# When a linear-attention scan may begin: beside its own head's projections, or after them

## The chip, the cores and the metric

The kernel runs on one core of one Trainium2 chip. The metric is device time in microseconds of one execution, taken as the median of several runs. Engines are named as in the profile: PE (TensorE, matmuls), DVE (VectorE), ACT (ScalarE), POOL (GpSimd) and SP (SyncE, which issues most of the DMAs).

## The reference

One layer of a hybrid decoder trunk in float32, for 2048 tokens of width 1024 with 16 learned meta tokens in front. One normalised input `u` feeds two branches, a Mamba-2 scan (SSD, four groups of heads) and a gated linear attention (GLA, four heads of key width 128 and value width 256). Two sigmoid gates merge them and an output matrix follows.

```python
u = rmsnorm(hres, norm_w)
proj = u @ w_in                              # z, xbc, dt, q, k, v, g_gla, a_lr, merge gates
# GLA branch, per head: o_t = q_t S_t,  S_t = diag(a_t) S_{t-1} + k_t^T v_t
log_a = log_sigmoid(a_lr @ gla_gate_w2 + gla_gate_b) / 16
o = rmsnorm(gla_chunked(q * 128**-0.5, k, v, log_a), gla_norm_w)
y_gla = o * silu(g_gla)
merged = sum over branches of sigmoid(gate) * (branch @ w_branch)
out = rmsnorm(hres + merged @ w_out, final_norm_w)[:, 16:]
```

In `gla_chunked` the queries, keys and decays alone make the decayed keys and queries and the attention matrix within a chunk. The values `v` are multiplied in only afterwards, and the output gate `g_gla` only at the very end.

## The kernel before

There are two phases. **Phase 1** walks over four blocks of 512 tokens (`for b in range(nblk)`, L812). In each block it works through eight units one after the other: four SSD groups (`ssd_proj`, then `ssd_scan`) and four GLA heads (`gla_proj`, then `gla_scan`). A unit's projections are the bulk of PE's work. Every product is done in three float32r matmuls, high by high, high by low and low by high (`accum`, L175 to L179). **Phase 2** (L837 on) does the merge gates, the branch products and the output product from stored tiles, as sums of seven sub-products (`product`).

Inside phase 1 the projections and the scans are Python generators. Each `yield` of a projection runs one step of every scan in flight (`step`, L798), in the order in which they were begun. PE and SP keep exactly the order in which the program was written (`manual_schedule`, L811). The order on DVE, ACT and POOL is chosen by the framework's scheduler. So on PE the matmuls of a scan's step stand between two pieces of projection.

`gla_proj` of a head has six steps: queries q (24 matmuls of 512 columns), keys k (24), values in two halves (48 matmuls of 256 columns each), and the two output gates (24 each). `gla_scan` has eleven:

- step 1 makes the decayed keys `kd` and queries `qg` and starts the first level (`level_in(64)`); it has nothing on PE;
- step 2 transposes `kd` (L699), then the first `level_out` (L681);
- steps 3 and 4 hold two `level_out` each, step 5 one more and the diagonal sums (L745); a `level_out` is a pair of matmuls into one PSUM bank, which ACT or DVE then copies out (L685, L688);
- step 6 transposes half of the attention matrix (L760); steps 7 and 8 take the four chunks (L769 to L776) with the values, the state `s_gla` and a norm;
- steps 9 to 11 scale, transpose (L786), multiply by the gates `gs` (L787) and store (L790).

PSUM has eight banks in phase 1: three in pool `pj` (projections), three in `pt` (transposes and sums) and **two in `pc`**. From `pc` come the banks of `level_out`, those of the GLA chunks, and in `ssd_scan` two for each chunk in `after(c)`: `py` (L545) and `pst` (L549). On DVE, L555 and then L558 read `py`, and L553 reads `pst`; after L558 and L553 the two banks are free.

`ssd_scan` of a group runs in eight steps beside the next unit. The scan of the fourth group therefore runs beside the first GLA head: its four `after(c)` come in steps 3 to 6 of that scan. In blocks 0 to 2, `fetch_u` (L290, L229 to L286) loads and normalises the next block's `u` from the first GLA head on. When all projections are done, `while running or begun: step()` (L824) drains the scans still in flight, and then phase 2 begins.

Of the kernel before, what the change touches and what calls it, by code (L numbers as in the profile page):

```python
# [17 lines left out]
META = 16  # L18
# [22 lines left out]
def trunk_kernel(ctx: ExitStack, tc: tile.TileContext, xm, xmt, w_feat, w_tok, w_zm, w_br, w_o,  # L41
                 cf32, cmsk, pvec, fnw, hvec, gw2, out):
    nc = tc.nc
# [5 lines left out]
    def mk(pool, shape, dt, tag, **kw):  # L49
        cnt[0] += 1  # L50
        return pool.tile(shape, dt, tag=tag, name=f"{tag}_{cnt[0]}", **kw)
# [73 lines left out]
    def bank(pool, tag):  # L125
        return mk(pool, [P, 512], F32, tag)
# [48 lines left out]
    def accum(ps, stat, mov, first, last, **kw):  # L175
        (sh, sl), (mh, ml) = stat, mov
        nc.tensor.matmul(ps, sh, mh, start=first, stop=False, **kw)  # L177
        nc.tensor.matmul(ps, sh, ml, start=False, stop=False, **kw)  # L178
        nc.tensor.matmul(ps, sl, mh, start=False, stop=last, **kw)  # L179

    def proj_feat(key, src, segs, moving):

        pss = [bank(pj, "pj") for _ in segs]
        for half in range(2):
            h, lo = load_w(f"{key}_{half}", src[:, half * 512:(half + 1) * 512])
            for k4 in range(4):
                kt = half * 4 + k4
                cs = slice(k4 * P, (k4 + 1) * P)
                for ps, (a, n) in zip(pss, segs):
                    accum(ps[:, :n], (h[:, cs], lo[:, cs]), moving(kt, a, n), kt == 0, kt == KT - 1)  # L190
        return pss

    def proj_tok(key, src, u, starts, banks, width=256, per=2, sub=None):

        nq = KT // per
        opened = set()
        for q0 in range(0, nq, 2):
            if q0 == nq // 2:  # L200
                yield
            ws = [load_w(f"{key}_{q}", src[:, q * per * width:(q + 1) * per * width]) for q in (q0, q0 + 1)]
            for i, ((bk, ps), a) in enumerate(zip(banks, starts)):
                c0 = sub if sub is not None and i >= NCH else 0
                for k2 in range(2 * per):
                    kt = q0 * per + k2
                    h, lo = ws[k2 // per]
                    cs = slice(k2 % per * width + c0, (k2 % per + 1) * width)
                    accum(ps[:, c0:width], tuple(t[:, kt, a:a + P] for t in u),
                          (h[:, cs], lo[:, cs]), bk not in opened, kt == KT - 1, skip_group_check=True)  # L210
                    opened.add(bk)

    def halves_of(pool, tag):

        bks = [bank(pool, tag) for _ in range(2)]
        return bks, [(i // 2, bks[i // 2][:, i % 2 * 256:(i % 2 + 1) * 256]) for i in range(4)]
# [7 lines left out]
    def split(h, lo, src):  # L224
        nc.scalar.activation(h, src, AF.Copy)
        nc.vector.tensor_tensor(lo, src, h.bitcast(F32), op=ALU.subtract)
# [101 lines left out]
    def new_block(b, u):  # L328
        o = Block()
        o.b, o.u = b, u  # L330
        o.m0 = META if b == 0 else 0
        o.tt = o.m0 + BLK
        o.segs_all = [(0, o.tt // 2), (o.tt // 2, o.tt // 2)] if b == 0 else [(0, BLK)]
        o.segs_real = [(o.m0, BLK)]
        o.starts = [o.m0 + c * P for c in range(NCH)]
        o.chunks = ([(0, META)] if o.m0 else []) + [(a, P) for a in o.starts]
        o.ci0 = 1 if o.m0 else 0
        o.nck = len(o.chunks)
        for nm in ("tkd", "tkc", "wde", "ecu", "dec"):
            setattr(o, nm, mk(bpool, [P, 5, NH], F32, nm, bufs=2))  # L340
        o.cumd = mk(dpool, [NH, BLK], F32, "cumd")
        o.g_all = mk(bpool, [P, GH, META + BLK], F32, "g_all")
        o.alr = mk(bpool, [P, 5, 48], F32, "alr")
        o.mov = lambda kt, a, n: tuple(t[:, kt, a:a + n] for t in u)
        return o
# [241 lines left out]
    def gla_proj(o, h):  # L587
        m0 = o.m0
        t0 = T_GLA + 4 * h
        qs = mk(wk, [P, META + BLK], F32, "act", bufs=NACT)  # L590
        ps, = proj_feat(f"g{t0}", w_feat[t0], o.segs_real, o.mov)
        nc.scalar.activation(qs[:, :BLK], ps, AF.Copy, scale=QSCALE)
        yield
        kf = mk(wk, [P, META + BLK], F32, "act", bufs=NACT)
        for ps, (a, n) in zip(proj_feat(f"g{t0 + 1}", w_feat[t0 + 1], o.segs_all, o.mov), o.segs_all):
            nc.scalar.activation(kf[:, a:a + n], ps[:, :n], AF.Copy)
        yield
        vh = mk(wk, [P, NCH, 256], F32R, "tok4", bufs=NT4)
        vl = mk(wk, [P, NCH, 256], F32R, "tok4", bufs=NT4)
        vm = None  # L600
        pss, places = halves_of(pj, "pj")
        if m0:
            vm = mk(wk, [P, 256], F32, "c1", bufs=NC1)[:META]
            pv5 = bank(pt, "pt")
            places.append((2, pv5[:, :256]))
        yield from proj_tok(f"v{h}", w_tok[SG + h], o.u, o.starts + [0] * o.ci0, places)
        if m0:
            nc.scalar.activation(vm, pv5[:META, :256], AF.Copy)
        for r, ps in enumerate(pss):
            split(*[t[:, 2 * r:2 * r + 2].rearrange("p c f -> p (c f)") for t in (vh, vl)], ps)  # L610
        yield
        gs = []
        for j in range(2):
            ps, = proj_feat(f"g{t0 + 2 + j}", w_feat[t0 + 2 + j], o.segs_real, o.mov)
            gg = mk(wk, [P, BLK], F32, "gg", bufs=4)
            nc.scalar.activation(gg, ps, AF.Tanh, scale=0.5)
            nc.vector.scalar_tensor_tensor(gg, gg, 1.0, ps, op0=ALU.add, op1=ALU.mult)
            gs.append(gg)
            yield
        begin(gla_scan(o, h, qs, kf, (vh, vl), vm, gs))  # L620

    def gla_scan(o, h, qs, kf, vt, vm, gs):
        m0, tt = o.m0, o.tt
        gf = o.g_all[:, h, :tt]
        gr = gf[:, m0:]
# [66 lines left out]
        if m0:  # L692
            ps = bank(pt, "pt")
            nc.tensor.transpose(ps[:META, :P], kd[:, :META], ident)
            btm = mk(wk, [P, P], F32, "bt")
            nc.scalar.activation(btm[:META], ps[:META, :P], AF.Copy)
        ps = bank(pt, "pt")
# [7 lines left out]
        yield  # L705
        if m0:
            ps = bank(pc, "pc")
            nc.tensor.matmul(ps[:, :256], btm[:META], vm, start=True, stop=True)
            nc.vector.tensor_copy(s_gla[:, h], ps[:, :256])
        level_out(32)  # L710
        level_in(8)
# [30 lines left out]
        for hl, n in parts:  # L742
            ps = bank(pt, "pt")
# [14 lines left out]
        ps = bank(pt, "pt")  # L758
# [6 lines left out]
        ssq = mk(sm, [P, 4], F32, "ssq")  # L765
        for c in range(NCH):
            po = bank(pc, "pc")
            vc = [t[:, c] for t in vt]
            accum(po[:, 256:], [t[:, c] for t in kdt], vc, True, True)  # L769
            accum(po[:, :256], [t[:, c] for t in atp], vc, True, False)  # L770
            nc.tensor.matmul(po[:, :256], qg[:, c * P:(c + 1) * P], s_gla[:, h], start=False, stop=True)
            nc.vector.scalar_tensor_tensor(s_gla[:, h], s_gla[:, h], egl[:, c:c + 1], po[:, 256:],
                                           op0=ALU.mult, op1=ALU.add)
            nc.scalar.activation(ot[:, c], po[:, :256], AF.Copy)
            jk = mk(wk, [P, 256], BF16, "junk", bufs=1)
            nc.scalar.activation(jk, po[:, :256], AF.Square, accum_out=ssq[:, c:c + 1])  # L776
            if c % 2:
                yield
# [4 lines left out]
        for j in range(2):  # L783
            ps = bank(pt, "pt")
# [10 lines left out]
    def begin(gen):  # L795
        begun.append(gen)
# [14 lines left out]
    with tc.manual_schedule(engines={mybir.EngineType.PE, mybir.EngineType.SP}):  # L811
        for b in range(nblk):  # L812
            o = new_block(b, next_u[b])
            for i in range(SG + GH):
                if (b, i) in beside:
                    begin(beside_unit(beside[b, i]))
                if i == 1:
                    begin(gates(o))
                if i == SG and b + 1 < nblk:
                    begin(fetch_u(b + 1))  # L820
                for _ in ssd_proj(o, i) if i < SG else gla_proj(o, i - SG):
                    step()
            save(0)
        while running or begun:  # L824
            step()
# [302 lines left out]
```

## Time and profile before

| | before |
|---|---|
| median of 3 runs | 2385.71 us (2382.58 to 2387.7) |
| profiled execution, span | 2382.4 us |
| PE busy | 2264.0 us (95%) |
| DVE busy | 1571.8 us (66%) |
| ACT busy | 1187.5 us (50%) |
| POOL busy | 680.0 us (29%) |
| mean granted TensorE clock | 0.976 |

For the profiled execution the page gives only its span, from the first to the last instruction; no time of its own beside it is listed, and the fastest of the three runs lies 0.2 us above the span. "Idle before" in a row of the trace is the time that an engine stood still just before that instruction, and the name behind it is what ended the wait. `x4` behind a row means that equal instructions that follow each other were merged. A matmul's end is modelled, so the start of the next row says more than the length of a row.

### The profile page before, as it was taken

What the parts mean: (1) busy time and instruction counts of PE and PEld (TensorE: products, weight loads), DVE (VectorE), ACT (ScalarE), POOL (GpSimd) and SP (SyncE); (2) the same over time, 40 slices, a digit from 0 to 9 for tenths busy, and PEclk for the clock granted to TensorE, in tenths of its full rate; (3) what the DMA queues carried; (4) which work ended last, traced back from release to release, by engine and by line L of the source; (5) the groups of instructions that cost most, each with busy time, mean ns of one, the idle gap of its engine ahead of it and who ended that gap; (6) DMA issues with size and microseconds to landing.
All of it is one profiled execution on the core that took longest, in us unless ns stands there. A gap on an engine that the chain in (4) does not pass through costs nothing. (4 is left out here: it accounts for less than half of the span.)

```text
span 2382.4 us, 36669 instructions
## 1 busy us (share of the span) xinstructions
PE 2264.0 (95%) x12641; PEld 1970.8 (83%) x12641; DVE 1571.8 (66%) x2889; ACT 1187.5 (50%) x2764; POOL 680.0 (29%) x681
## 2 busy tenths in 40 slices
PE   6899999999999999999999999789989999998998
PEld 6889989888889988888989889668877788877786
DVE  4676665676675676676666655764757855786976
ACT  4665655465544455544455534364634445553443
POOL 3343433122222122321122100324433454332431
PEclk8999999999999999999999999789999999999999
DMA  8665875667786676786666654364777965787652
GB/s 271 213 209 193 293 240 190 225 201 235 245 276 184 215 220 220 258 267 199 208 213 212 205 167 143 131 217 136 263 248 264 313 198 173 251 264 225 231 177 106
DMA packets 301547, 518.07 MB, mean 217 GB/s; under 512 B 27696, under 2 KB 143664, under 8 KB 301360
## 3 DMA queue, kind: packets, MB, share of 16 engines
q1 hardware_dynamic: 231856, 452.66, 58.2%
q10 hardware_dynamic: 69504, 63.06, 8.0%
q8 instruction: 99, 1.62, 0.3%
q14 instruction: 88, 0.72, 0.1%
HBM read 368.42 MB, written 147.19 MB: 216 GB/s over the span
## 5 line engine op out<-in xcount | busy, mean ns | idle before, releaser
L177 PE MATMUL pj<-u,whl 128*128 128x512 f32 (+1 forms) x1184 | 447.4, 378 | 9.3 <-ACT g_all L420 3.3
L179 PE MATMUL pj<-u,whl 128*128 128x512 f32 (+1 forms) x1184 | 431.5, 364 | 0.8 <-POOL whl L165 0.8
L178 PE MATMUL pj<-u,whl 128*128 128x512 f32 (+1 forms) x1184 | 430.9, 364 | 0.0
L177 PE MATMUL pj<-whl,u 128*128 128x256 f32 (+1 forms) x992 | 289.9, 292 | 8.7 <-ACT u L282 6.1
L179 PE MATMUL pj<-whl,u 128*128 128x256 f32 (+1 forms) x992 | 284.1, 286 | 1.3 <-DVE u L284 1.3
L177 PE MATMUL psa<-b,a 128*128 128x512 f32 x640 | 255.5, 404 | 30.8 <-ACT sn L913 20.6
L178 PE MATMUL pj<-whl,u 128*128 128x256 f32 (+1 forms) x992 | 283.8, 286 | 0.7 <-POOL whl L165 0.5
L177 PEld LDWEIGHTS pj<-u,whl 128*128 128x128 f32 x1184 | 225.7, 191 | 47.1 <-ACT g_all L420 3.7
L179 PE MATMUL psa<-b,a 128*128 128x512 f32 x640 | 255.8, 400 | 2.3 <-DVE a L897 2.2
L179 PEld LDWEIGHTS pj<-u,whl 128*128 128x128 f32 x1184 | 225.2, 190 | 36.7 <-POOL whl L165 1.1
L178 PE MATMUL psa<-b,a 128*128 128x512 f32 x640 | 255.5, 399 | 0.0
L178 PEld LDWEIGHTS pj<-u,whl 128*128 128x128 f32 x1184 | 225.8, 191 | 33.2
L876 DVE TENSOR_TENSOR b<-br,b 128x512 fp32r<-128x512 f32 x196 | 160.8, 842 | 59.3 <-ACT b L875 58.9
L177 PEld LDWEIGHTS pj<-whl,u 128*128 128x128 f32 x992 | 191.0, 193 | 9.7 <-ACT u L282 6.6
L179 PEld LDWEIGHTS pj<-whl,u 128*128 128x128 f32 x992 | 191.2, 193 | 2.1 <-DVE u L284 2.1
L178 PEld LDWEIGHTS pj<-whl,u 128*128 128x128 f32 x992 | 191.1, 193 | 2.0 <-POOL whl L165 1.6
L897 DVE TENSOR_TENSOR a<-ar,a 128x512 fp32r<-128x512 f32 x160 | 136.2, 855 | 83.1 <-ACT a L896 82.6
L80 POOL TENSOR_TENSOR wr<-wr 128x256 f32<-128x256 f32 x80 | 66.2, 828 | 430.9 <-DMA wr<-y 173.0
L165 POOL TENSOR_TENSOR whl<-wr,whl 128x512 fp32r<-128x512 f32 (+1 forms) x100 | 132.7, 1334 | 191.6 <-ACT whl L164 166.3
L875 ACT ACTIVATE b<-br 128x512 fp32r<-128x512 f32 x196 | 119.8, 627 | 133.4 <-DMA br<-br_t 35.4
L177 PEld LDWEIGHTS psa<-b,a 128*128 128x128 f32 x640 | 124.9, 195 | 61.8 <-ACT sn L913 24.1
L462 DVE SCALAR_TENSOR_TENSOR acc<-cin,hcw,acc 128x512 f32<-128x512 f32 (+1 forms) x192 | 156.3, 814 | 26.8 <-ACT acc L458 26.1
(267 smaller groups left out, 5025.1 us busy)
## 6 DMA issues: line engine op xcount, KB each, us to landing
whl<-k_s SPq DMA_DIRECT2D x96, 512.0 KB, 4.5
whl<-k_g SPq DMA_DIRECT2D x96, 512.0 KB, 4.2
whl<-k_v SPq DMA_DIRECT2D x48, 512.0 KB, 3.9
whl<-k_z SPq DMA_DIRECT2D x36, 512.0 KB, 3.7
wr<-in_w_feat SPq DMA_DIRECT2D x64, 256.0 KB, 4.4
k_s<-whl SPq DMA_DIRECT2D x32, 512.0 KB, 3.5
cb<-cumd ACTq DMA_DIRECT2D x64, 256.0 KB, 5.7
y<-gg ACTq DMA_DIRECT2D x64, 256.0 KB, 4.6
```

The lines of the kernel that those rows point to most:

```text
L80: nc.gpsimd.tensor_tensor(o, x, y, op=ALU.subtract)
L165: nc.gpsimd.tensor_tensor(hl[:, 1], raw, hl[:, 0].bitcast(F32), op=ALU.subtract)
L177: nc.tensor.matmul(ps, sh, mh, start=first, stop=False, **kw)
L178: nc.tensor.matmul(ps, sh, ml, start=False, stop=False, **kw)
L179: nc.tensor.matmul(ps, sl, mh, start=False, stop=last, **kw)
L462: nc.vector.scalar_tensor_tensor(acc, cin[:, k:k + tt], hcw[:, ti, k:k + 1], acc, op0=ALU.mult, op1=ALU.add)
L875: nc.scalar.activation(t[:, 0], raw, AF.Copy)
L876: nc.vector.tensor_tensor(t[:, 1], raw, t[:, 0].bitcast(F32), op=ALU.subtract)
L897: nc.vector.tensor_tensor(t[:, 1], src, t[:, 0].bitcast(F32), op=ALU.subtract)
```

## The change

The scan of a head is begun right behind the keys instead of behind the output gates. The scan's generator receives a dictionary `values`, which is filled when the values have been projected, and a list `gs`, which is filled when the gates have been projected. `begin` is called five steps earlier, so that steps 1 to 5 of a scan run beside its own head's k, v, v, g, g, and steps 6 to 11 beside the next unit. Nothing is computed differently.

```diff
         kf = mk(wk, [P, META + BLK], F32, "act", bufs=NACT)
         for ps, (a, n) in zip(proj_feat(f"g{t0 + 1}", w_feat[t0 + 1], o.segs_all, o.mov), o.segs_all):
             nc.scalar.activation(kf[:, a:a + n], ps[:, :n], AF.Copy)
+        values, gs = {}, []
+        begin(gla_scan(o, h, qs, kf, values, gs))
         yield
...
             split(*[t[:, 2 * r:2 * r + 2].rearrange("p c f -> p (c f)") for t in (vh, vl)], ps)
-        yield
-        gs = []
+        values.update(vt=(vh, vl), vm=vm)
+        yield
         for j in range(2):
...
             gs.append(gg)
             yield
-        begin(gla_scan(o, h, qs, kf, (vh, vl), vm, gs))
-
-    def gla_scan(o, h, qs, kf, vt, vm, gs):
+
+    def gla_scan(o, h, qs, kf, values, gs):
...
-            nc.tensor.matmul(ps[:, :256], btm[:META], vm, start=True, stop=True)
+            nc.tensor.matmul(ps[:, :256], btm[:META], values["vm"], start=True, stop=True)
...
-            vc = [t[:, c] for t in vt]
+            vc = [t[:, c] for t in values["vt"]]
```

Below L600 the changed kernel's lines are one higher (L681 becomes L682, L699 becomes L700, L745 becomes L746, L760 becomes L761). The first place is PE in block 1, inside the first GLA head, between the second half of the values (ahead) and the first output gate (behind). L523 to L550 belong to chunks 1 and 2 of the fourth SSD group. Before:

```order
L523 MATMUL pt_7599<-cst,act_7017 128x128
L523 MATMUL pt_7599<-cst,act_7097 128x128
L523 MATMUL pt_7599<-cst,act_7181 128x128
L547 MATMUL pc_7617<-c_1230_7496,sq_7503 128x64 x4
L548 MATMUL pc_7617<-s_ssd,act_7261 128x256
L550 MATMUL pc_7623<-c_1231_7498,bt_7501 128x256
L177 MATMUL pj_7652<-u_2935,whl_7653 128x512
```

With the change, at the same place:

```order
L523 MATMUL pt_7650<-cst,act_7017 128x128
L523 MATMUL pt_7650<-cst,act_7097 128x128
L523 MATMUL pt_7650<-cst,act_7181 128x128
L547 MATMUL pc_7668<-c_1237_7518,sq_7525 128x64 x4
L548 MATMUL pc_7668<-s_ssd,act_7261 128x256
L550 MATMUL pc_7674<-c_1238_7520,bt_7523 128x256
L682 MATMUL pc_7703<-sq_7573 128x128 x2
L682 MATMUL pc_7715<-sq_7585 128x128 x2
L177 MATMUL pj_7727<-u_2935,whl_7728 128x512
```

Two `level_out` now stand right behind L548 and L550, and each of them writes one of the two `pc` banks that those have just filled. The same happens with one `level_out` in the step ahead of this one (behind L699's transposes), with two in the step behind it and with one in the step after that.

The second place is DVE one step ahead of that, around the release of chunk 0's banks (L555, L558 and L553). L248 and L250 belong to `fetch_u`. Before:

```order
L538 TENSOR_TENSOR sq_7503<-sq_7503,sq_7394 128x512
L538 TENSOR_TENSOR sq_7610<-sq_7610,sq_7394 128x512
L666 TENSOR_TENSOR sq_7851<-g_all_5181 128x512
L248 TENSOR_TENSOR ss_7640<-ss_1258_7641 128x1
L555 TENSOR_TENSOR c_1236_7520<-pc_7510,ecu_5178 128x256
L553 TENSOR_TENSOR s_ssd<-s_ssd,pc_7516 128x256
L250 TENSOR_SCALAR rs_1261_7649<-ss_7640 128x1
L558 TENSOR_TENSOR c_1236_7520<-c_1236_7520,pc_7510 128x256
```

With the change:

```order
L672 TENSOR_TENSOR sq_7573<-sq_7572,act_7342 128x8x32
L674 TENSOR_TENSOR sq_7573<-sq_7572,act_7283 128x2x2x32 x2
L555 TENSOR_TENSOR c_1243_7542<-pc_7532,ecu_5385 128x256
L538 TENSOR_TENSOR sq_7525<-sq_7525,sq_7394 128x512
L667 TENSOR_TENSOR sq_7584<-g_all_5388 128x512
L248 TENSOR_TENSOR ss_7691<-ss_1273_7692 128x1
L553 TENSOR_TENSOR s_ssd<-s_ssd,pc_7538 128x256
L558 TENSOR_TENSOR c_1243_7542<-c_1243_7542,pc_7532 128x256
```

The scheduler had drawn the first part of `level_in` (L666), which needs only queries, keys and decays, into this head's projections before, too: four L666 stand between L509 and this head's second gate, and six L667 now. The decay products of the SSD chunks (L538) ran one or two chunks ahead before and stand right at their own chunk now. From L509 to the second gate (L617, now L619) the list of DVE has 75 rows with the change and 54 before.

The third place is PE at the end of phase 1, behind the last projection (`pj_17106`, the last head's second gate). The changed kernel:

```order
L179 MATMUL pj_17106<-u_11321,whl_17121 128x512
L682 MATMUL pc_17140<-sq_17077 128x128 x2
L746 MATMUL pt_17144<-c_2937_17098,ones_r 128x256
L746 MATMUL pt_17144<-c_2938_17099,ones_r 128x256
L746 MATMUL pt_17147<-sq_17102,ones_r 128x512
L746 MATMUL pt_17147<-sq_17103,ones_r 128x512
L761 MATMUL pt_17158<-cst,sq_17151 128x128 x2
```

Before, this stretch came only after the following, which ends the third head's scan and begins the fourth's; ahead of these rows stand the third head's L760 and its four chunks:

```order
L699 MATMUL pt_17032<-cst,act_16986 128x128 x4
L681 MATMUL pc_17049<-sq_17001 128x128 x2
L681 MATMUL pc_17068<-sq_17042 128x128 x2
L681 MATMUL pc_17080<-sq_17054 128x128 x2
L786 MATMUL pt_17092<-cst,ot_16960 128x128 x4
L786 MATMUL pt_17098<-cst,ot_16960 128x128 x4
L681 MATMUL pc_17104<-sq_17073 128x128 x2
L681 MATMUL pc_17116<-sq_17085 128x128 x2
```

All of that now stands among the last head's projections.

## The prediction

> **What bounds the kernel now.** I read the page first, then the busy time by stretches, then the rows of PE around the places where the change puts or removes something.
>
> ```profile
> PE 2264.0 (95%) x12641; PEld 1970.8 (83%) x12641; DVE 1571.8 (66%) x2889; ACT 1187.5 (50%) x2764; POOL 680.0 (29%) x681
> ```
>
> PE is busy for 95% of the span, so on average it is the bound. The stretches (length, then busy time of PE, PEld, DVE, ACT and POOL, granted clock, DMA share, GB/s) show where it is not:
>
> ```profile
> 1340.00:1508.00 168.00, 168.00 (x1035) 150.88 (x1034) 90.78 (x215) 66.73 (x178) 13.10 (x12) 1.00 0.52 169
> 1508.35:1538.84 30.49, 16.18 (x67) 12.87 (x66) 29.13 (x54) 15.56 (x43) 14.18 (x10) 0.72 0.27 86
> 1508.00:1557.00 49.00, 28.20 (x119) 21.63 (x117) 37.11 (x69) 21.73 (x62) 15.54 (x11) 0.71 0.20 65
> 622.00:668.00 46.00, 43.83 (x272) 39.35 (x273) 29.31 (x70) 25.03 (x70) 12.99 (x17) 1.00 0.82 267
> 637.00:641.00 4.00, 2.89 (x21) 2.79 (x22) 2.62 (x5) 0.96 (x2) 1.96 (x3) 1.00 0.79 218
> ```
>
> From 1340 to 1508 us, the GLA heads of the last block, PE never stands still. Then comes the drain: 49 us with 28.2 of PE and a clock of 0.71. There the bound is the chain from DVE and ACT to PE and back. The stretch from 622 to 668 is the first GLA head of block 1, where the scan of the fourth SSD group runs beside the projections: PE 43.8 of 46, DVE 29.3.
>
> So the change removes time from a drain that happens once, and adds steps to a place that comes four times and where PE is the bound. These two I price.
>
> **The drain.** The last projection, the first matmul of the fourth head's last `level_out`, and the first of phase 2:
>
> ```profile
> 1508.12 0.39 PE L179 MATMUL pj<-u,whl 128*128 128x512 f32 x1
> ...
> 1538.84 0.85 PE L681 MATMUL pc<-sq 128*128 128x128 f32 x4 [3.32 <-DVE c L688]
> ...
> 1557.16 1.22 PE L177 MATMUL psa<-b,a 128*128 128x512 f32 x2 [1.88 <-ACT b L875]
> ```
>
> A 512-column matmul takes 0.23 (the rows at 716.82 and 717.06 below), so the drain lasts from 1508.35 to 1557.16, 48.8 us. The rows from 1538.84 on are the tail of step 5 and steps 6 to 11 of the fourth head, 18.3 us. That is all that is left to drain after the change. Its DVE work will run beside the preparation of phase 2 on POOL, which now falls into the last projections and the drain's beginning. What that costs shows in one row:
>
> ```profile
> 1506.34 1.77 DVE L666 TENSOR_TENSOR sq<-g_all 128x512 f32<-128x512 f32 x1
> ```
>
> The mean of this operation is 0.793 (next fence). One or two operations of the remaining chain slowed by 1 us make about 1.5, so the drain is 20 us, and 28.8 go away. The 67 matmuls between 1508.35 and 1538.84 do not vanish, they now stand among projections. They have 256 columns at most, so at 0.23 for 512 they take 67 x 0.12 = 8; at most 16.18 x 0.72 = 11.7, the busy time scaled to full clock. Net: −28.8 + 8 to 9 = **−20**, between −14 (11.7 moved, three more slowed operations) and −24 (none slowed, part of the moved work in gaps of PE).
>
> **The first head of each block.** Two `level_out` behind L550 want the two `pc` banks that L547 to L550 have just filled. PE keeps its order, so everything behind them waits too: 24 matmuls of a projection, and through them ACT and DVE. When do the banks come free today? PE first, then DVE, of block 1's first (639.54, 644.11) and last chunk (663.06, 666.67) of four, and of the quickest place that I found (865.98, 867.38):
>
> ```profile
> 638.11 1.10 PE L547 MATMUL pc<-c,sq 128*128 128x64 f32 x8 [1.63 <-DVE sq L538]
> ...
> 639.54 0.59 PE L550 MATMUL pc<-c,bt 128*128 128x256 f32 x2
> ...
> 663.06 0.59 PE L550 MATMUL pc<-c,bt 128*128 128x256 f32 x2
> ...
> 865.98 0.59 PE L550 MATMUL pc<-c,bt 128*128 128x256 f32 x2
> ```
>
> ```profile
> 644.11 0.41 DVE L553 TENSOR_TENSOR s_ssd<-s_ssd,pc 128x256 f32<-128x256 f32 x1
> ...
> 666.67 0.41 DVE L558 TENSOR_TENSOR c<-c,pc 128x256 f32<-128x256 f32 x1
> ...
> 867.38 0.41 DVE L558 TENSOR_TENSOR c<-c,pc 128x256 f32<-128x256 f32 x1
> ```
>
> L550 occupies PE for about 0.25. In the first chunk L553 ends at 644.52, 4.7 after PE is through; L699 and a part of the pair cover 0.6, which leaves a wait of 4.1. In the last chunk L558 ends at 667.08, 3.8 after, and 3.5 are left. With the two chunks between (4.9 and 2.4, worked out likewise) a block waits 14.9, four blocks 60. The quickest place gives 867.79 − 866.23 = 1.6, less 0.4 covered; about 1 on average over a chunk's step, 4 a block, 16 in all. I take 10 a block, **+40**, the middle: while PE stands still DVE catches up, but DVE also gets more to do. How much:
>
> ```profile
> L699 PE MATMUL pt<-cst,act 128*128 128x128 f32 x64 | 9.9, 279 | 3.8 <-ACT gg L583 2.1 <-DVE act L639 1.7
> ...
> L638 ACT ACTIVATE act<-g_all,gl 128x128 f32<-128x128 f32 x64 | 20.4, 390 | 0.0
> L670 ACT ACTIVATE sq<-sq 128x256 f32<-128x256 f32 x96 | 39.2, 408 | 0.0
> ...
> L666 DVE TENSOR_TENSOR sq<-g_all 128x512 f32<-128x512 f32 x96 | 76.1, 793 | 0.5
> L673 DVE TENSOR_TENSOR sq<-sq,act 128x128 f32<-128x128 f32 x192 | 57.1, 336 | 0.0
> L671 DVE TENSOR_TENSOR sq<-sq,act 128x256 f32<-128x256 f32 x96 | 49.1, 512 | 7.5 <-PE pc L681 6.2
> L688 DVE COPY_PREDICATED c<-msk,pc 128x256 f32<-128x256 uint8 x80 | 35.3, 441 | 41.8 <-PE pc L681 41.7
> ```
>
> Of the 21 rows that DVE has more up to the second gate, two are L666 (1.6), three L671 (1.5), three pairs L673 (2.0) and four L688 (1.8), 6.9 together; the remaining nine are products and splits, twelve instructions of an estimated 0.5 by the nearest of these means, 6. With 29.3 busy before that is 42 of 46: full, but not over.
>
> **The first chunk's wait.** L547 waits 1.63 for L538 at 638.11, and L538 for ACT's exponent L537. The change puts up to four L638 (1.56) and one level's exponents (twice 0.41, pricing L669 as L670) ahead of that on ACT: 2.4, less what ACT idles. In addition the decay products no longer run a chunk ahead. I take 1.5 a block, **+6**, between 0 and 14 (3.5 a block).
>
> **The clock.** A longer wait costs more than itself:
>
> ```profile
> 713.37 1.22 PE L771 MATMUL pc<-s_gla,act 128*128 128x256 f32 x2 [2.89 <-DVE s_gla L772]
> 714.02 0.99 PE L177 MATMUL pj<-u,whl 128*128 128x512 f32 x1
> ...
> 716.82 0.40 PE L177 MATMUL pj<-u,whl 128*128 128x512 f32 x1
> 717.06 0.40 PE L178 MATMUL pj<-u,whl 128*128 128x512 f32 x1
> ```
>
> After a wait of 2.89 seven matmuls from 714.02 to 716.82 took 2.80 instead of 7 x 0.24 = 1.7, and with the L771 pair ahead of them about 1.5 was lost. After the wait of 1.63 at 638.11 the clock stayed at 1.00 (the stretch 637 to 641). At a mean wait of 2.5, I let 9 of the 16 be long enough: 9 x 1.5 = **+14**, between 0 and 16 x 1.5 = 24. The Trainium skill, "TensorE: Matmul & The Clock Gate", section "Part 1: The HAM clock gate (the "warmup" mystery)", says that the clock halves after at least one idle window of about 3.4 us, which runs freely. By it a wait of 2.89 would leave the clock alone; the row at 714.02 speaks against that.
>
> **What goes.** L699's waits (3.8 in the whole trace) and a few of L771 get other neighbours: **−4**, between −6 and 0. A scan issues DMAs only in its last step, two stores from ACT's queue (L790), now five steps earlier; no wait of PE in phase 1 hangs on them, and SP's weight loads keep their places. The values are projected one step ahead of nothing that needs them: they are used in step 7, two steps after the gates, so this edit costs nothing.
>
> **The sum.** 40 + 6 + 14 − 4 − 20 = +36. The profiled execution's span is 2382.4, which makes 2418.4; the median of the runs lies 3.3 above that span (2385.7), which makes **2422**.
>
> **The rivals.**
>
> *The banks come free in time* (the other side). If DVE takes L555, L558 and L553 at once, as at 865.98, the place costs 16 in four blocks and no clock. With −24 to −30 from the drain and from what goes, and 0 to 6 for the first chunks, that is −14 to −2: 2372 to 2384. It decides where the 16 waits average under (20 + 4 − 6) / 16 = 1.1 us and the clock holds. For it: the last block has no `fetch_u` on DVE. Against it: in block 1 every release came 2.4 us or more late with a lighter DVE. 0.15.
>
> *DVE becomes the bound in the first heads.* With 42 of 46 us, and an order in which decay products stand ahead of the releases, all four blocks could wait as block 1 does or more: 60, 24 for the clock, 14 for the first chunks, less 4 and 14 = +80, 2466. Against it: DVE's load beside PE was never over 90% for long in these stretches. 0.12.
>
> *A wait costs only its own length.* If waits of 2 to 5 us do not lower the clock except for two or three, 14 becomes 4: 2412. That is what the rule of "TensorE: Matmul & The Clock Gate" in the Trainium skill would give. For it: most waits are under 3.4. Against it: the row of 714.02. 0.20.
>
> *The drain does not shrink,* because the fourth head's chain is as late as it was: +56, 2442. Against it: the order of PE has only one `level_out` and steps 6 to 11 behind the last projection, and DVE is busy for 91 of the 168 us before. 0.03.
>
> **How the numbers follow.** The forecast of 2422 keeps 0.50. The range goes from 2374 to 2460: it holds the forecast with 4 to 15 a block, the case of the clock, the drain, and most of the case of freed banks; left out is most of the case with DVE as the bound and the lowest end. About 0.2%, 4.8 us, is what a measurement can tell here. Faster: 0.11 of the freed banks and 0.02 of the forecast's own spread, 0.13. Same: 0.04 and 0.01, 0.05. Slower: the rest, 0.82.
>
> **What would show each step.** In the changed profile the drain from the last L179 on `pj` to the first `psa` should be 18 to 24 us. The pairs L682 in each block's first GLA head should show waits of 1 to 5 us with DVE's `c` or `s_ssd` (L558, L553) as releaser, some 10 us a block, and rows that follow each other at 0.42 instead of 0.23 behind the longer ones. L700 should wait hardly at all. The prediction is wrong if these pairs wait under 1 us or for something else, if the stretch of the first heads grows by over 20 us a block, or if phase 2 starts later by more than the waits say.

## The result, and the profile after

The changed kernel takes 2413.6 us (median of 4 runs, 2407.4 to 2419.4), the kernel before 2384.1 beside it: a ratio of 1.0121, 95% interval 1.0099 to 1.0144. It is slower, by 29.5 us. The profiled execution is the slowest of the four (2419.4); its span, from the first to the last instruction, is 2417.6, 4.0 above the median. Against the span of before (2382.4) that is +35.2, and this difference is what the trace can be asked about.

The page of the changed kernel:

```profile
PE 2273.8 (94%) x12641; PEld 1975.1 (82%) x12641; DVE 1554.5 (64%) x2889; ACT 1188.2 (49%) x2764; POOL 694.9 (29%) x681
```

The number of instructions is the same, DVE is busy for a smaller share than before, and PE is busy for 10 us more. The busy time by stretches says where. Each of the four rows is the GLA part of a block, in blocks 0 to 2 with the next block's first units, beside which the fourth head's scan still runs. The rows are cut at the same projection matmuls in both kernels (stretch, length, busy time of PE, PEld, DVE, ACT, POOL, granted clock, DMA share, GB/s). Before:

```profile
244.88:554.60 309.72, 303.73 (x1961) 272.38 (x1961) 205.52 (x426) 173.15 (x439) 95.05 (x94) 1.00 0.68 229
617.38:893.90 276.52, 269.23 (x1645) 239.67 (x1644) 178.23 (x398) 135.42 (x352) 56.50 (x75) 0.99 0.73 229
996.21:1270.96 274.75, 268.36 (x1667) 239.51 (x1665) 181.12 (x400) 137.64 (x359) 53.91 (x72) 1.00 0.70 224
1342.64:1507.89 165.25, 165.25 (x1023) 148.61 (x1021) 88.35 (x211) 66.47 (x177) 12.38 (x11) 1.00 0.52 169
```

After; the fifth row is the drain:

```profile
245.62:573.40 327.78, 310.14 (x1962) 277.33 (x1962) 205.68 (x427) 174.31 (x441) 96.81 (x94) 0.98 0.66 216
636.17:927.48 291.31, 275.46 (x1646) 243.60 (x1645) 176.29 (x399) 136.10 (x354) 59.58 (x74) 0.98 0.68 217
1033.26:1320.32 287.06, 272.33 (x1666) 240.65 (x1665) 177.84 (x400) 136.17 (x354) 60.67 (x72) 0.99 0.67 214
1392.08:1575.26 183.18, 176.84 (x1089) 157.57 (x1088) 103.88 (x257) 76.87 (x212) 17.56 (x14) 0.99 0.49 154
1575.49:1596.78 21.29, 11.07 (x52) 8.71 (x50) 13.51 (x22) 10.42 (x28) 9.98 (x8) 0.78 0.41 135
```

The four stretches grew by 18.1, 14.8, 12.3 and 17.9, together 63.1 us. Of this PE stands still for 34.9 (length less PE busy, after less before) and is busy for 28.2 more, although it does only the moved matmuls in addition, and those in the last row alone. The drain shrank from 48.8 to 21.3.

What PE waits for there, by the view of waits (total us, times, longest):

```profile
PE pc L682 <- DVE s_ssd L553: 19.3, 10, 4.8
PE pc L682 <- DVE c L558: 10.5, 5, 3.7
...
PE pc L709 <- DVE c L558: 2.0, 1, 2.0
```

The first two lines are 29.8 us in 15 waits of `level_out`, all in the first head of a block, and all for the two instructions that free the SSD chunk's banks. The third is a sixteenth wait of the same kind: in block 0 the matmul of the meta tokens (L709) wants such a bank. The four places of block 1 on PE:

```profile
657.51 0.59 PE L550 MATMUL pc<-c,bt 128*128 128x256 f32 x2
...
663.38 1.22 PE L682 MATMUL pc<-sq 128*128 128x128 f32 x4 [4.84 <-DVE s_ssd L553]
...
676.08 2.04 PE L682 MATMUL pc<-sq 128*128 128x128 f32 x8 [1.53 <-DVE s_ssd L553]
...
688.37 1.16 PE L682 MATMUL pc<-sq 128*128 128x128 f32 x8 [1.04 <-DVE s_ssd L553]
...
698.98 0.68 PE L682 MATMUL pc<-sq 128*128 128x128 f32 x4 [2.21 <-DVE c L558]
```

And DVE, from L550 to the end of the first of these waits:

```profile
659.36 0.43 DVE L672 TENSOR_TENSOR sq<-sq,act 128x256 f32<-128x256 f32 x1 [2.34 <-ACT sq L670]
659.71 1.43 DVE L674 TENSOR_TENSOR sq<-sq,act 128x128 f32<-128x128 f32 x2
661.06 0.41 DVE L555 TENSOR_TENSOR c<-pc,ecu 128x256 f32<-128x256 f32 x1
661.63 0.69 DVE L538 TENSOR_TENSOR sq<-sq,sq 128x512 f32<-128x512 f32 x1 [0.16 <-ACT sq L537]
662.24 0.69 DVE L667 TENSOR_TENSOR sq<-g_all 128x512 f32<-128x512 f32 x1
662.84 0.15 DVE L248 TENSOR_TENSOR ss<-ss 128x1 f32<-128x1 f32 x1
662.91 0.41 DVE L553 TENSOR_TENSOR s_ssd<-s_ssd,pc 128x256 f32<-128x256 f32 x1
```

DVE stands still for 2.34 us at L672, for ACT's exponent of a level; 0.8 of that lies within PE's wait. For nearly all the rest of PE's wait DVE does what stands in its queue ahead of the release. The two L674 among this took 0.81 and 0.69 us, where the median of L674 is 0.28; POOL was at work beside them. ACT in turn was at `fetch_u`:

```profile
657.94 0.63 ACT L247 ACTIVATE acc<-acc 128x512 f32<-128x512 f32 x1 [0.61 <-DMA acc<-in_xm]
...
658.92 0.42 ACT L670 ACTIVATE sq<-sq 128x256 f32<-128x256 f32 x1 [0.25 <-ACT acc L247]
```

So the chain of the 4.84 us is: a square of the next block's input waits 0.61 us for its DMA and takes 0.63, behind it on ACT the exponent L670, behind that on DVE the level's products, the decay product, the start of another level, and only then the release. Behind the wait the clock is low:

```profile
664.62 0.41 PE L178 MATMUL pj<-whl,u 128*128 128x256 f32 x1
664.83 0.41 PE L179 MATMUL pj<-whl,u 128*128 128x256 f32 x1
...
669.31 0.29 PE L179 MATMUL pj<-whl,u 128*128 128x256 f32 x1
669.44 0.28 PE L177 MATMUL pj<-whl,u 128*128 128x256 f32 x1
```

0.21 us from one 256-column matmul to the next until 669.3, 0.12 from there on. The granted clock (the share of full speed that the throttle lets PE have, behind the POOL figures) shows the same, first for most of the wait, then for what follows it:

```profile
659.09:662.50 3.41, 0.00 (x0) 0.00 (x0) 2.98 (x6) 2.08 (x7) 1.82 (x3) 1.00 0.91 308
662.50:669.33 6.83, 5.95 (x28) 5.95 (x29) 3.32 (x11) 3.15 (x10) 0.66 (x1) 0.50 0.23 83
```

The end of phase 1:

```profile
1575.26 0.39 PE L179 MATMUL pj<-u,whl 128*128 128x512 f32 x1
1575.48 0.60 PE L682 MATMUL pc<-sq 128*128 128x128 f32 x4
...
1581.60 0.69 PE L761 MATMUL pt<-cst,sq 128*128 128x128 f32 x2 [4.81 <-DVE sq L754]
...
1592.66 2.11 PE L787 MATMUL pt<-cst,ot 128*128 128x128 f32 x8 [3.19 <-ACT ot L782]
1596.78 0.80 PE L177 MATMUL psa<-b,a 128*128 128x512 f32 x1 [2.00 <-ACT b L876]
```

One head's tail is left there, with the waits of its own chain.

### The profile page after: what moved, and what is told of

It reads as the page before. It is cut to its first block, busy times and chain, and to the rows that moved or that the text cites. A ratio compares the mean times of both kernels' runs of the same rounds, so it can differ in the third digit from the quotient of the medians.

```text
span 2417.6 us, 36659 instructions
## 1 busy us (share of the span) xinstructions
PE 2273.8 (94%) x12641; PEld 1975.1 (82%) x12641; DVE 1554.5 (64%) x2889; ACT 1188.2 (49%) x2764; POOL 694.9 (29%) x681
## 5 line engine op out<-in xcount | busy, mean ns | idle before, releaser
L898 DVE TENSOR_TENSOR a<-ar,a 128x512 fp32r<-128x512 f32 x160 | 137.3, 862 | 79.0 <-ACT a L897 76.3
L462 DVE SCALAR_TENSOR_TENSOR acc<-cin,hcw,acc 128x512 f32<-128x512 f32 (+1 forms) x192 | 159.4, 830 | 34.9 <-ACT acc L458 33.6
```

The costliest lines, as they stand in the source:

```text
L462: nc.vector.scalar_tensor_tensor(acc, cin[:, k:k + tt], hcw[:, ti, k:k + 1], acc, op0=ALU.mult, op1=ALU.add)
L898: nc.vector.tensor_tensor(t[:, 1], src, t[:, 0].bitcast(F32), op=ALU.subtract)
```

## The experiments

Each time stands beside the kernel before on the same chip: 2382.2 us (first four runs), 2382.6 (next four) and 2384.0 (last four). The theory was that `level_out` collides with the fourth SSD group's chunks over two PSUM banks, once in each block, and that the drain gains once.

**Other banks for `level_out`** (`e1_lvl_pt`)

```diff
             kq = kqs.pop(half)
-            ps = bank(pc, "pc")
+            ps = bank(pt, "pt")
```

> The changed kernel, but the bank of each level_out comes from pool pt (three banks) instead of pc (two). Theory (the cost lies in level_out wanting the two banks that the SSD chunk has just filled): the waits of L682 for L553 and L558, 31 us in the changed kernel, and the loss of clock behind them, some 16 us, go, while the drain stays at 21 us: 2414 - 47 = 2367, between 2358 and 2380. Rival (DVE and ACT are late in the first heads whatever the banks): the wait moves to the next matmul that needs DVE, and the time stays between 2400 and 2416.

2383.7 us, ratio 1.0008 (0.9994 to 1.0021): 28 us less above the kernel before than with the change, but 17 more than expected, and outside both expectations. No wait of L682 for L553 or L558 is left. Something else came late instead, in the view of waits:

```profile
PE pt L746 <- ACT c L225: 4.4, 3, 2.3
PE pt L746 <- DVE c L226: 4.2, 3, 1.6
```

These are the diagonal sums of step 5, in the first heads of blocks 0 to 2. The cost up to the last projection is 35.3 us instead of 67.1, and 9.7 of that is moved work (below). The theory holds for the L682 waits; the time was missed, because the next late thing was not counted.

**The change in the last block only, ramped in** (`e2_ramp_last`)

```diff
+        late = (5, 4, 2, 0)[h] if o.b == nblk - 1 else 5   # steps after the keys
...
+            if n == 1 + late:
+                begin(scan.pop())
```

> The kernel before in blocks 0 to 2. In the last block the four heads' scans begin 0, 1, 3 and 5 steps earlier than before, so that only the last one begins right behind its keys, and none meets the fourth SSD group's chunks any more than before (the first not at all). Theory: the drain shrinks from 49 to about 21 us, the 8 us of moved matmuls are paid among the projections, and no first head pays: 2384 - 20 + 2 = 2366, between 2360 and 2374. Rival (the gain in the drain is given back among the last head's projections): 2378 to 2386.

2374.1 us, 0.9964 (0.9950 to 0.9977): faster than before, by 8 instead of 18, at the edge of the range. The drain is 21.9 us. But consecutive GLA scans, now begun four or five steps apart instead of six, meet in `pc`, where `level_out` waits 3.8 us in the last block and did not wait before. The last block's GLA part is 15.4 us longer, 5.7 more than the moved work.

**Only the first head of each block early** (`e3_h0_only`)

```diff
+        late = 0 if h == 0 else 5
```

> The scan begins early in the first GLA head of each block alone, in the other heads as before. Theory (the cost is where the GLA scan meets the fourth SSD group's): the whole cost without the drain's gain, 31 us of waits, some 16 of clock and a little else, so 2384 + 50 = 2434, between 2422 and 2445, and a drain of 49 us. Rival (the cost is spread over all heads, because DVE and ACT get their work in another order): about a quarter of it, 2392 to 2402.

2426.0 us, 1.0172 (1.0129 to 1.0214). The time is in the range of the theory. Most of the cost sits in the first heads: +46.7 us at the last projection, where no work was moved past it; the changed kernel has 67.1, or 57.4 without the moved work. The drain is about as long as before:

```profile
1555.07:1602.75 47.68, 26.39 (x118) 20.60 (x116) 35.93 (x67) 20.82 (x60) 15.00 (x11) 0.73 0.21 68
```

**Work in the waits** (`e4_fill`, again as `e10_fill_again` beside the changed kernel as `e9_after_again`)

```diff
+            if h == 0 and half in (64, 32, 8, 2):
+                pf = bank(pt, "pt")
+                for i in range(10):
+                    nc.tensor.matmul(pf[:, :P], kq[:, :P], kq[:, P:2 * P], start=True, stop=True)
             ps = bank(pc, "pc")
```

> The changed kernel with ten additional 128x128 matmuls of about 0.2 us, whose result is not used, ahead of the first level_out of steps 2 to 5 in each block's first head, in a bank of pool pt: 16 x 2 = 32 us more for PE, most of it where PE stands still now. Theory (the waits themselves lower the clock): about 27 of the 32 us lie in the waits, and 10 to 16 us of clock come back: 2414 + 5 - 13 = 2406, between 2398 and 2414. Rival (the clock falls for another reason, or the waits only move behind the added work): 2418 to 2446.

> The changed kernel once more, on the same chip as the three below, to have their differences from it and not from a run on another day. It was 29.5 us above the kernel before: 2408 to 2418 is expected.

> The kernel with the ten added matmuls (32 us more for PE) once more, beside the changed kernel on the same chip, because its phase 1 was 11 us shorter in the profile while the median was the same. Theory (the waits lower the clock, and work in them costs nothing): 0 to 12 us below the changed kernel. Rival (the clock is not the waits' doing): 5 to 30 above it.

2414.1 us the first time. The second time 2419.2 (1.0139, 1.0121 to 1.0156) beside 2414.8 for the changed kernel (1.0136, 1.0118 to 1.0154). The medians lie between the two expectations, and the ratios are equal: the added matmuls cost nothing that the runs can tell. They had been priced at 32 us and take 36 in the traces (each of the 160 stands there as two rows of 0.11 to 0.12). The sums over the four stretches, changed kernel first, then filled:

```profile
sum 1088.82, PE 1033.83 PEld 917.69 DVE 663.57 ACT 522.95 POOL 235.76; mean PE 258.46 PEld 229.42 DVE 165.89 ACT 130.74 POOL 58.94
```

```profile
sum 1086.97, PE 1059.39 PEld 948.83 DVE 662.99 ACT 524.21 POOL 237.35; mean PE 264.85 PEld 237.21 DVE 165.75 ACT 131.05 POOL 59.34
```

Idle time falls from 55.0 to 27.6 us, 27 as expected. PE is busy for 25.6 more, although 36 were added: 11 us came back in this pair, and 15.5 in the first (busy +20.4 against the first profile of the changed kernel). The record of the granted clock agrees: the time lost to half clock in the four stretches falls from 15.4 to 7.3 us in this pair, and from 17.3 to 2.0 in the first. The clock's part is thus shown in the traces of two runs, 8 and 15 us where 10 to 16 were expected; the time alone would not show it.

**The change in the last block only, whole** (`e5_last_pc`), **and there with other banks** (`e6_last_pt`)

```diff
+        late = 0 if o.b == nblk - 1 else 5
...
-            ps = bank(pc, "pc")
+            ps = bank(pt, "pt") if o.b == nblk - 1 else bank(pc, "pc")     # e6 only
```

> The change in the last block alone, with level_out's banks from pc as in the change; blocks 0 to 2 as before. Theory (each block pays for itself, the drain gains once): the last block pays the 10 us that it pays in the changed kernel, with 8 us of moved matmuls, the drain loses 27 to 28: 2382 - 10 = 2372, between 2367 and 2377. Rival (the drain's gain needs the whole change, or the blocks pay one for the other): over 2380.

> As the run with the change in the last block alone, but there the banks of level_out come from pool pt. Theory: in the last block 2.6 us remain of the cost (the run with all banks from pt), so 2382 - 17 = 2365, between 2360 and 2370. Rival (the waits of the last block are hidden anyway, and banks do not matter there): the same as with pc, 2372.

2370.3 us (0.9948, 0.9930 to 0.9966) and 2365.7 (0.9926, 0.9907 to 0.9946), both within 2 us of the theory. **Both beat both kernels**, the second by more: 16.9 us less than before. Its last block and its drain (the profiled execution was the fastest of its six, 2357.8):

```profile
1341.40:1517.23 175.83, 174.98 (x1088) 156.79 (x1087) 102.53 (x257) 76.69 (x212) 17.78 (x14) 1.00 0.49 161
1517.46:1539.09 21.63, 11.41 (x51) 9.05 (x49) 13.08 (x22) 10.29 (x28) 9.17 (x8) 0.77 0.39 132
```

With the clock at 1.00 and PE idle for 0.9 us, the last block takes 175.8 instead of 165.3. The busy time of PE, 174.98 less 165.25, is the moved work by itself: 9.7 us.

**Control: other banks without the change** (`e7_before_pt`; the edit of the first experiment in the kernel before)

> The kernel before, but level_out's banks come from pool pt. Control for the run with all banks from pt. Theory (banks matter only where level_out meets the SSD chunk): no change, 2382, between 2377 and 2386. Rival (pt is the better pool for level_out anywhere, or the worse one): 5 us or more away from 2382 on either side.

2388.5 us, 1.0019 (1.0003 to 1.0035). The median is beyond the 5 us of the rival, on the slow side, and the theory's range is missed by 2.5. The trace does not show where: phase 2 begins at 1556.3 (1557.2 before) and then takes 818 us to its last matmul instead of 815. In any case pool `pt` is not better by itself, and the first experiment's gain is due to the collision.

**`fetch_u` one head later** (`e8_fetch_later`)

```diff
-                if i == SG and b + 1 < nblk:
+                if i == SG + 1 and b + 1 < nblk:
                     begin(fetch_u(b + 1))
```

> The changed kernel with fetch_u, the load and normalisation of the next block's input, begun with the second GLA head of a block instead of the first. In the changed kernel blocks 0 to 2 pay 15 to 18 us and the last, which has no fetch_u, 10. Theory (fetch_u's work on DVE and ACT beside the first head makes the difference): blocks 0 to 2 fall to 10 to 12 each, 2414 - 14 = 2400, between 2394 and 2408. Rival (it does not matter): 2410 to 2418, or more where the input then comes too late for the next block.

2397.8 us, 1.0055 (1.0033 to 1.0077), as the theory had it. What is left of the waits:

```profile
PE pc L682 <- DVE s_ssd L553: 17.3, 10, 2.2
...
PE pc L682 <- DVE c L558: 4.6, 5, 1.7
```

In blocks 1, 2 and 3 the four waits are now 6.3, 5.6 and 5.5 us; with `fetch_u` beside them they were 9.6, 6.8 and 5.5. The last block never had a `fetch_u`: 5.5 is what the collision's waits come to without it.

**Both remedies in all blocks** (`e11_pt_fetch_later`; the edits of the first and of the last experiment)

> The changed kernel with both remedies: level_out's banks from pt, and fetch_u begun with the second head. From pt 27 us remained of the first heads' cost, 24 of them in blocks 0 to 2, where L746 waits for splits that DVE and ACT do late. Theory (that remainder is fetch_u's work beside the first head): half of the 24 go, 2384 - 12 = 2372, between 2364 and 2378. Rival (the remainder is the other heads' or the pool's): 2380 to 2390.

2371.2 us, 0.9950 (0.9930 to 0.9969), as expected. Of the 8.6 us of L746's waits 1.9 are left: `fetch_u` had been in their way too.

**The GLA step ahead of the SSD step** (`e12_gla_first`)

```diff
-        begin(gla_scan(o, h, qs, kf, values, gs))
+        if h == 0:
+            running.insert(0, gla_scan(o, h, qs, kf, values, gs))
+        else:
+            begin(gla_scan(o, h, qs, kf, values, gs))
```

> The changed kernel, but in each block's first head the GLA scan takes its step ahead of the fourth SSD group's, so that level_out comes first and L547 and L550 want the banks behind it. Theory (a level_out's bank is free after one copy of 0.44 us on DVE, the SSD chunk's after three operations and a product on POOL): about half of the waits go, 2414 - 18 = 2396, between 2386 and 2406. Rival (it is DVE's queue that is late, whichever bank it is): 2406 to 2420.

2386.0 us, 1.0011 (0.9995 to 1.0028): 10 us better than the theory, at the lower edge of its range. The banks are the same two, and the work is the same. Only the order of the pieces inside a step is turned (the GLA scan's goes ahead of all others in flight, so ahead of `fetch_u`'s too), and `level_out` now gets banks that were freed a whole projection ago. L547 and L550 now want banks that a single copy frees, and wait 12 us in all instead of L682's 30 (and L547's 3.5), more than half of it in two waits for a copy on ACT:

```profile
PE pc L550 <- ACT c L689: 6.5, 2, 4.2
```

## Why the prediction was right

The median came 8 us below the forecast of 2422, in the range and on its side; on the profiled execution the forecast was 2418.4 and the span 2417.6. So close a hit is partly luck, as the terms show: one came out smaller than forecast, one larger.

| term | predicted | measured (span after less before) |
|---|---|---|
| waits for the two banks, first chunk, what goes | 40 + 6 − 4 = 42 | 34.9 idle time, 31.8 of it the banks |
| clock | 14 | 28.2 − 9.7 = 18.5 longer busy time (granted clock: 15.2) |
| drain, with the moved work | −20 | −27.5 + 9.7 = −17.8 |
| rest of phase 1 | 0 | 4.0 |
| phase 2 | 0 | −4.4 |
| sum | 36 | 35.2 |

*The banks.* The mechanism is shown four times: by the releasers, with other banks (`e1_lvl_pt`, no such waits), with the first heads alone (`e3_h0_only`, 46.7 of 57.4 us) and in the other order (`e12_gla_first`). The size was between the two ends, 8 us a block instead of 10, from 5.5 in the last block to 9.9 in block 0. The prediction took the middle on the argument that DVE catches up while PE stands still, and this is what the rows show: 4.84 for the first chunk of block 1, where 4.1 had been read off, then 1.53 and 1.04, where 4.9 and 2.4 had been.

*The first chunk.* Mis-sized: L547 waits 1.40 and 1.69 in blocks 1 and 2, and 1.63 and 1.32 before. What L638 adds on ACT did not reach L547, so 6 should have been near 0.

*The clock.* Nine low stretches were forecast; between 266 and 1435 us nine are there, seven behind a wait of L682, one behind L709's for L558 and one behind a wait for weights, outside the four rows. By the spacing of their rows they cost the projections 14 us, as forecast. The record of the granted clock gives the four rows as a whole: 34.6 us at half clock, 4.2 before, so 17.3 us lost instead of 2.1, and 15.2 for the change. The other 3.3 us of longer busy time are not explained. The rival by which a wait costs only its length falls: the clock went down after waits of 2.52, 1.98, 2.21 and 2.23 us. Its time, 2412, is nearer to the median than the forecast, so the trace decides here and not the time. The Trainium skill, in "TensorE: Matmul & The Clock Gate", section "A second HAM failure mode: psum-queue depth-cycling", tells of a kernel that lost its clock by cycling through PSUM banks; this trace agrees, with 15.2 us.

*DVE as the bound* falls too. The first head of block 1:

```profile
640.90:707.50 66.60, 55.58 (x311) 48.91 (x311) 42.81 (x102) 33.61 (x92) 14.39 (x18) 0.90 0.60 195
```

DVE is busy for 42.8 us, which is what was summed (42), but of 66.6. Its queue is late at the release without being full: part of the time it waits for ACT, and that link the prediction did not see. It priced ACT's queue for L537 only, and named `fetch_u` only for its DVE instructions. `e8_fetch_later` puts some 15 us on `fetch_u`, its work on ACT and on DVE together; no run parts the two.

One sign that the prediction named as speaking against it did show: the first head was to grow by no more than 20 us a block, and grew by 23.1, 18.4, 15.7 and 12.1. Part of that is the moved scan steps, which now run there.

*The banks in time*, the rival on the other side, needed an average wait under 1.1 us. It was 2.0 in the changed kernel. The times that it names were reached only by other edits, about 2371 in `e11_pt_fetch_later` and 2386 in `e12_gla_first`.

*The drain.* 21.3 us where 20 were forecast. The remaining chain did meet the preparation of phase 2, as row 1506.34 had suggested, in the wait of L761 (4.81, and 1.45 before). DVE there:

```profile
1577.53 1.71 DVE L751 TENSOR_TENSOR sq<-c,cst 128x512 f32<-128x512 f32 x1
1579.17 1.74 DVE L898 TENSOR_TENSOR a<-ar,a 128x512 fp32r<-128x512 f32 x1
1580.84 0.71 DVE L754 COPY_PREDICATED sq<-msk,pt 128x512 f32<-128x512 uint8 x1
```

L751 took 1.71 instead of 0.69 while POOL was busy, the forecast slowdown. Not forecast was L898, an operation of phase 2 that the scheduler put into the chain: 1.7 us more. The moved work was 9.7, between the 8 taken and the bound of 11.7.

*Open:* why phase 2 lasts 807 to 818 us to its last matmul in the profiled runs, with the same instructions; the kernels with the order of before (815 and 818) and the changed ones (807 to 817) overlap. The 4.4 us of the table are within that, and not a result of the change that is shown. The 4.0 in the rest of phase 1 lie mostly ahead of block 2's row, where PE waited 2.69 for the weights `k_g`, 1.2 before, and had a low clock behind it; no run tested it.

## What to carry to other kernels

Before a chain is started earlier, look at what it will stand behind on the in-order engine: here a matmul that wants a PSUM bank waited hardly at all a projection after the bank was filled, and 0.6 to 4.8 us right behind it, although no engine is full. A gain that comes once (the drain) and a cost that comes with each block must be weighed by their counts; here the change pays if it is made only where the drain is, in the last block (12 us, or 17 with other banks). Where two pieces share few banks inside a step, try their order first (29 us here), then another pool (28 us).

## What was not expected of the hardware

The clock does not follow the length of a wait alone. In the changed kernel it fell after waits of 1.93 and, seven microseconds after another low stretch, of 1.53 us, and held after 1.97, 1.76 and 1.53. It held after 2.77 in the first filled run and after 3.07 where the change was made in the last block alone. Behind the seven waits of 3.18 to 4.84 us in the GLA parts of these runs it always fell.

The traces' record of the granted clock shows what it does follow. In all fourteen traces it is 1.00 or 0.50, and it changes only on a grid of 3.41 us that runs on through the whole execution; 659.09, 662.50 and 669.33 above are points of it. Take the steps of this grid between 245 and 2300 us that have full clock, and count how long PE stood still within each. Behind all 150 steps with 1.95 us or more the clock was low in the next step, behind none of the 7902 with less than 1.4, and behind 29 of the 112 between. So a wait of 3.07 us that the grid cuts into 1.87 and 1.20 is let pass, and one of 1.56 us that lies whole within a step lowered the clock (at 343.3 us in `e9_after_again`). In the changed kernel's nine low stretches the clock was low for one or two steps, 3.41 or 6.83 us, and the projections in them lost 1.0 to 2.3 us.
